# Residual add and RMSNorm: three shared slots of six rows in a hardware loop in place of two slots of eight rows unrolled

## The chip, the cores and the metric

The kernel runs on one core of one Trainium2 chip. The metric is the device time of one execution in microseconds (us). Every byte comes from the chip's memory (HBM) and goes back to it; the other cores are idle.

## The reference

```python
def reference(x, residual, gamma, eps):
    z = x + residual
    rms = np.sqrt(np.mean(z ** 2, axis=-1, keepdims=True) + eps)
    return (z / rms * gamma).astype(np.float32)
```

`x` and `residual` are float32 of 32 x 2048 x 2048, that is 65,536 rows of 2,048 numbers (8 KiB a row). The two inputs are 1,073.7 MB and the output is 536.9 MB. `gamma` is one row, all ones in the inputs used, but read and multiplied in.

## The kernel before, in words

The rows are cut into 64 tiles of 1,024 rows. Each of the 128 partitions of the on-chip memory (SBUF) takes 8 neighbouring rows of a tile, 64 KiB. There are three slots of that size: two, `z0` and `z1`, for x, z and the result in place, used in turn, and one, `r_slot`, for residual. With gamma (8 KiB) that is 200 KiB a partition.

One queue, that of SyncE (SP), issues all large transfers: residual of a tile whole (L58), x in two halves of four rows (L64), the store whole (L69), that of the last tile in halves (L73). The instructions of one queue are issued in program order, and each waits for its semaphores before it is issued, so one that waits holds up all behind it.

VectorE (DVE) adds four rows at once (L80). ScalarE (ACT) squares each row and sums it (L83), then takes the root (L90). VectorE inverts it (L94) and multiplies each row by it and by gamma (L97). The order in the main loop, unrolled by Python into one straight program, is: store of tile i-1, compute of tile i, residual of i+1, x of i+1. Residual can be loaded when both adds of the tile before are done; x when the store that empties its slot has landed.

## Time and profile before

| | |
|---|---|
| median of 10 runs | 3734.39 us (3733.63 to 3734.95) |
| profiled execution, its own time | 3735.05 us |
| its span, first to last instruction | 3733.3 us |
| bytes moved by the DMA engines | 1610.82 MB, mean 431 GB/s |
| busy: VectorE, ScalarE | 62%, 29% |
| q1, the queue issued from SP | 99.9% of 16 engines' span |

The page gives, for one profiled execution, each engine's busy time, the work of 40 equal slices, the DMA queues, the chain of work that ended last, and the costliest groups of instructions. In a group's row stand line, engine, operation and shapes, then busy time in us and the mean of one in ns, then the idle time ahead of it and what ended most of it. The view of waits gives for each waiting line who released it: us in total, times, longest. Behind the page lie the records of single DMA packets: start, duration, size. A packet here is one partition's share of one transfer; a transfer has 128, eight on each of the 16 DMA engines, and ends with one small semaphore write by each engine.

### The profile page before, as it was taken

How to read it: one execution, taken by the hardware profiler on the slowest of the kernel's cores; microseconds unless marked ns; L12 is line 12 of the kernel's file. 1: busy time of each engine (PE TensorE's matmuls, PEld its weight loads, DVE VectorE, ACT ScalarE, POOL GpSimd, SP SyncE). 2: the span in 40 equal slices, each digit the busy share in tenths (PEclk: the TensorE clock that was granted, in tenths of full speed). 3: DMA queues.
4: the chain of work that ended last, by engine and by line, in shares of the span. 5: the costliest groups of instructions: out<-in, count | busy, mean ns of one | idle time of the engine just before them, and what ended most of it. 6: DMA issues, size and time to landing. Idle time of an engine off the chain costs nothing.

```text
span 3733.3 us, 2427 instructions
## 1 busy us (share of the span) xinstructions
DVE 2297.9 (62%) x772; ACT 1066.0 (29%) x1154; POOL 0.2 (0%) x4
## 2 busy tenths in 40 slices
DVE  5665755657557565575655756657566575665756
ACT  2331322313223132231322313323233232331322
POOL 0000000000000000000000000000000000000000
DMA  9999999999999999999999999999999999999999
GB/s 424 413 433 431 434 436 430 436 432 434 434 430 438 432 433 433 430 437 432 433 434 431 436 432 432 437 429 436 431 433 435 431 436 433 430 436 434 433 435 388
DMA packets 37035, 1610.82 MB, mean 431 GB/s; under 512 B 4116, under 2 KB 4116, under 8 KB 4116
## 3 DMA queue, kind: packets, MB, share of 16 engines
q1 hardware_dynamic: 37008, 1610.63, 99.9%
q14 instruction: 19, 0.16, 0.0%
q10 hardware_dynamic: 8, 0.03, 0.0%
HBM read 1073.77 MB, written 536.87 MB: 431 GB/s over the span
## 4 chain that ended last, share of the span: by engine, by line
DMA 66%; another core or an unknown queue 16%; DVE 16%; SPq 1%; ACT 0%; issue 0%; DVEq 0%
DMA z<-in_x_dram 64%; DVE z L80 15%; DMA out_dram<-z 1%; DVE z L97 1%; DMA r_slot<-in_residual_dram 1%; SPq L64 1%; SPq L58 0%; ACT sq_junk L83 0%; DVE rstd L94 0%; DVEq L158 0%; ACT L90 0%; ACT rms L90 0%; DVEq L80 0%
## 5 line engine op out<-in xcount | busy, mean ns | idle before, releaser
L80 DVE TENSOR_TENSOR z<-z,r_slot 128x8192 f32<-128x8192 f32 x128 | 1112.5, 8692 | 1395.6 <-DMA z<-in_x_dram 1382.7
L83 ACT ACTIVATE sq_junk<-z 128x2048 f32<-128x2048 f32 x512 | 963.5, 1882 | 2636.0 <-DVE z L80 2623.9
L97 DVE SCALAR_TENSOR_TENSOR z<-z,rstd,gamma_tile 128x2048 f32<-128x2048 f32 x512 | 1169.9, 2347 | 4.5
L83 ACT ACTIVATION_READ_ACCUMULATOR sq_junk<-z 128x1 f32 x512 | 95.5, 186 | 0.0
L90 ACT ACTIVATE rms<-ssq,eps_tile 128x4 f32<-128x4 f32 x128 | 38.1, 297 | 4.1
L94 DVE RECIPROCAL rstd<-rms 128x4 f32<-128x4 f32 x128 | 21.8, 171 | 0.1
L113 DVE LOAD_MASK_SELECT gamma_tile<-gamma_tile x1 | 0.0, 14 | 21.3 <-DMA gamma_tile<-in_gamma_dram 21.3
L83 ACT ACT_TABLE_LOAD x1 | 1.3, 1283 | 4.4 <-issue 4.4
L113 DVE STREAM_SHUFFLE gamma_tile<-gamma_tile 128x2048 f32<-128x2048 f32 x1 | 2.4, 2418 | 0.0
L108 DVE MEMSET gamma_tile<- 128x2048 f32 x1 | 1.8, 1765 | 0.4 <-issue 0.4
L90 ACT ACT_TABLE_LOAD x1 | 1.3, 1283 | 0.0
L55 DVE MEMSET eps_tile<- 128x1 f32 x1 | 0.1, 59 | 0.8 <-PEq L144 0.8
L144 POOL MEMSET const-uint8-127<- 128x1 uint8 x1 | 0.1, 103 | 0.0
L144 POOL MEMSET const-bfloat16-1.0<- 128x1 bf16 x1 | 0.1, 102 | 0.0
L144 POOL MEMSET const-float32-0.0<- 128x1 f32 x1 | 0.1, 99 | 0.2 <-issue 0.2
L144 POOL MEMSET const-float32-1.0<- 128x1 f32 x1 | 0.1, 99 | 0.0
## 6 DMA issues: line engine op xcount, KB each, us to landing
z<-in_x_dram SPq DMA_DIRECT2D x128, 4096.0 KB, 38.3
out_dram<-z SPq DMA_DIRECT2D x2, 4096.0 KB
r_slot<-in_residual_dram SPq DMA_DIRECT2D x64, 29.9
out_dram<-z SPq DMA_DIRECT2D x63, 50.1
gamma_tile<-in_gamma_dram ACTq DMA_DIRECT2D x4, 8.0 KB
```

What stands on the lines that cost most here:

```text
L55: nc.vector.memset(eps_tile, float(eps))
L64: nc.sync.dma_start(out=z[:, s, :], in_=x_t[i][:, s, :])
L80: nc.vector.tensor_add(out=z[:, s, :], in0=z[:, s, :], in1=r_slot[:, s, :])
L83: nc.scalar.activation(out=sq_junk, in_=z[:, h * H + g, :], func=Act.Square, accum_out=ssq[:, g : g + 1],)
L90: nc.scalar.activation(out=rms, in_=ssq, func=Act.Sqrt, bias=eps_tile, scale=inv_d)
L94: nc.vector.reciprocal(out=rstd, in_=rms)
L97: nc.vector.scalar_tensor_tensor(out=row, in0=row, scalar=rstd[:, g : g + 1], in1=gamma_tile, op0=mult, op1=mult,)
L108: nc.vector.memset(gamma_tile, 0.0)
L113: nc.vector.stream_shuffle(gamma_tile, gamma_tile, [0] * 32)
L144: nc = _bacc.Bacc("TRN2", target_bir_lowering=False, num_devices=1)
```

## The change

- **Slots and tiles.** Four slots of 48 KiB a partition in place of three of 64 KiB: three (`z0` to `z2`) for x, z and result, one for residual. A tile is 768 rows, six a partition. 65,536 rows are 85 such tiles and 256 rows over; these make a first tile of two rows a partition. Its residual goes into `z2`, which is free then, so that tile 1's residual can go into `r_slot` at once.
- **Transfers.** x is loaded whole. Only the last tile is cut: its residual, its compute and its store go in three pieces of two rows.
- **Order.** For each tile: store of i-1, x of i+1, compute of i, residual of i+1. x is no longer behind residual on SP.
- **Compute.** Adds take three rows at once (128x6144), in two groups; roots and reciprocals are of three values.
- **A loop of the hardware.** Tiles 2 to 82 run in `For_i`, three tiles a pass, 27 passes. Addresses in HBM come from registers. With `iteration_sync="reg_based"` the loop's semaphores are never set back: each pass compares them with registers that grow by what one pass adds. Nine transfers in the body count on eight semaphores in turn, so DMAHW0 is used by the first (the store, L88) and the ninth (residual, L91). There is no barrier between passes; when the loop is left, SP waits for all transfers and all engines meet at one.

In the program as built, the first store of the body waits for DMAHW0 to hold 32 for every pass gone by (16 for each of the two transfers that count on it), beside VectorE's count for the rows scaled. The instructions of SP in the body are:

```
L88 DMACopy out_0_dram<-z1_65 128x12288 [waits DMAHW3,DMAHW0,DMAHW4,DVE,DMAHW6]
L89 DMACopy z0_64<-in_x_dram 128x12288 [waits DMAHW1]
L91 DMACopy r_slot_67<-in_residual_dram 128x12288 [waits DMAHW2,DVE]
L88 DMACopy out_0_dram<-z2_66 128x12288 [waits DMAHW0,DMAHW7,DVE]
L89 DMACopy z1_65<-in_x_dram 128x12288
L91 DMACopy r_slot_67<-in_residual_dram 128x12288 [waits DMAHW5,DMAHW2,DVE]
L88 DMACopy out_0_dram<-z0_64 128x12288 [waits DMAHW3,DMAHW1,DVE]
L89 DMACopy z2_66<-in_x_dram 128x12288
L91 DMACopy r_slot_67<-in_residual_dram 128x12288 [waits DMAHW5,DVE]
```

(Waits on semaphores of before the loop, which have been met since, and register instructions are left out.)

```diff
-    R = 8
-    H = R // 2
+    R = 6
+    NZ = 3
+    n_full = n_rows // (P * R)
+    left = (n_rows - n_full * P * R) // P
+    sizes = ([left] if left else []) + [R] * n_full
...
-    stats = ctx.enter_context(tc.tile_pool(name="stats", bufs=3))
+    stats = ctx.enter_context(tc.tile_pool(name="stats", bufs=6))
...
-    z_slots = [slots.tile([P, R, D], fp32, name=f"z{k}") for k in range(2)]
+    z_slots = [slots.tile([P, R, D], fp32, name=f"z{k}") for k in range(NZ)]
...
+    last = n_tiles - 1
+    piece = 2
+
+    def pieces(i):
+        k = sizes[i]
+        return [(a, min(a + piece, k)) for a in range(0, k, piece)] if i == last else [(0, k)]
+
+    def r_of(i):
+        return z_slots[NZ - 1] if i == 0 else r_slot
...
+    def cycle(i, at):
+        z_next = z_slots[(i + 1) % NZ]
+        nc.sync.dma_start(out=o_full[at - 1], in_=z_slots[(i - 1) % NZ])
+        nc.sync.dma_start(out=z_next, in_=x_full[at + 1])
+        compute(i)
+        nc.sync.dma_start(out=r_slot, in_=r_full[at + 1])
+
+    def load_x(i):
+        nc.sync.dma_start(out=z_slots[i % NZ][:, : sizes[i], :], in_=rows(x_f, i))
+
     def load_r(i):
-        nc.sync.dma_start(out=r_slot, in_=r_t[i])
-
-    def load_x(i):
-        z = z_slots[i % 2]
-        for h in range(2):
-            s = slice(h * H, (h + 1) * H)
-            nc.sync.dma_start(out=z[:, s, :], in_=x_t[i][:, s, :])
+        for a, b in pieces(i):
+            nc.sync.dma_start(out=r_of(i)[:, a:b, :], in_=rows(r_f, i)[:, a:b, :])
 
     def store(i):
...
+        for a, b in pieces(i):
+            nc.sync.dma_start(out=rows(o_f, i)[:, a:b, :], in_=z_slots[i % NZ][:, a:b, :])
...
     def compute(i):
...
+        if i == last:
+            before = None
+            for a, b in pieces(i):
+                add(i, a, b)
+                rms = square(i, a, b)
+                if before is not None:
+                    scale(i, *before)
+                before = (a, b, rms)
+            scale(i, *before)
             return
...
+        groups = [(a, min(a + 3, sizes[i])) for a in range(0, sizes[i], 3)]
+        rms_of = []
+        for a, b in groups:
+            add(i, a, b)
+            rms_of.append(square(i, a, b))
+        for (a, b), rms in zip(groups, rms_of):
+            scale(i, a, b, rms)
...
+    load_x(0)
     load_r(0)
-    load_x(0)
     load_gamma()
     load_x(1)
+    load_r(1)
     compute(0)
-    load_r(1)
-    for i in range(1, n_tiles):
+    def turn(i):
         store(i - 1)
+        if i + 1 < n_tiles:
+            load_x(i + 1)
         compute(i)
         if i + 1 < n_tiles:
             load_r(i + 1)
-            load_x(i + 1)
-    store(n_tiles - 1)
+
+    lo = 2
+    n_loop = (last - 1 - lo) // NZ
+    for i in range(1, lo):
+        turn(i)
+    with tc.For_i(0, n_loop * NZ, NZ, iteration_sync="reg_based") as iv:
+        for c in range(NZ):
+            cycle(lo + c, iv + (lo + c - first_full))
+    for i in range(lo + n_loop * NZ, n_tiles):
+        turn(i)
+    store(last)
```

The helpers `add`, `square` and `scale` hold what L80, L83 to L90 and L94 to L97 did, on rows a to b of a tile (L106, L112 and L119, L127 and L130 after).

## The prediction

> **What bounds the kernel now.** I read the page's head, its DMA rows, and the busy time by windows.

> ```profile
> span 3733.3 us, 2427 instructions
> DVE 2297.9 (62%) x772; ACT 1066.0 (29%) x1154; POOL 0.2 (0%) x4
> ...
> DMA  9999999999999999999999999999999999999999
> ...
> q1 hardware_dynamic: 37008, 1610.63, 99.9%
> ```

> The only full resource is the 16 DMA engines: q1's packets take 99.9% of their span. VectorE is busy 62%, ScalarE 29%. The windows view (length, busy time and instructions of each engine, clock, DMA share, GB/s; packets are counted where they start) says where the transfers stop:

> ```profile
> 163.38:3654.16 3490.78, 2150.01 (x721) 997.10 (x1080) 0.00 (x0) 1.00 1.00 433
> 100.20:101.80 1.60, 1.56 (x3) 1.40 (x4) 0.00 (x0) 1.00 0.01 0
> 3704.00:3712.00 8.00, 7.96 (x6) 6.46 (x9) 0.00 (x0) 1.00 0.13 57
> ```

> In 3490.78 us of steady state the share is 1.00 at 433 GB/s. There are two holes, at 100 us and ahead of the last stores. The second costs nearly nothing: by the trace's packet records one of the 16 engines lags further and further, ends the store of tile 62 at 3712.27 us and starts the last tile's at once, while the others have been idle since 3703.6 to 3710.9. The span is that engine's unbroken work. So what matters is any moment at which *all* engines have nothing queued. SP is the only issuer of these transfers, and its own waits are hidden behind transfers already queued:

> ```profile
> SPq L58 <- DVE rstd L94: 1772.7, 63, 29.5
> SPq L58 <- DMA r_slot<-in_residual_dram: 678.6, 62, 12.5
> SPq L64 <- DMA out_dram<-z: 625.7, 62, 10.5
> SPq L69 <- DVE z L97: 465.4, 63, 18.3
> ```

> The last row is the important one: the store (L69) waits for the scaled rows, never for a load.

> [...]

> **The change part by part.**

> *Bytes and packets.* Bytes are the same, 1610.63 MB. A 65,536-byte packet takes 2418 ns in the packet records, a 32,768-byte one 1213.5: about 9 ns plus 37.6 ns per KiB. So a 48 KiB packet should take 1816 ns. One tile before: 16 packets of 2418 and 16 of 1213.5 per engine, and four 9 ns semaphore writes, 58.14 us; times 64, 3721.0. After: three transfers of 8 x 1816 + 9, 43.61 us, times 85, 3706.9, plus 14.7 for the two-row tile, 3721.6. Difference +0.6; I take 0 (from -3 to +4, as packet times vary a little).

> *VectorE and ScalarE.* The costliest groups (line, engine, shapes, count; busy us, mean ns of one; idle before):

> ```profile
> L80 DVE TENSOR_TENSOR z<-z,r_slot 128x8192 f32<-128x8192 f32 x128 | 1112.5, 8692 | 1395.6 <-DMA z<-in_x_dram 1382.7
> L83 ACT ACTIVATE sq_junk<-z 128x2048 f32<-128x2048 f32 x512 | 963.5, 1882 | 2636.0 <-DVE z L80 2623.9
> L97 DVE SCALAR_TENSOR_TENSOR z<-z,rstd,gamma_tile 128x2048 f32<-128x2048 f32 x512 | 1169.9, 2347 | 4.5
> ```

> An add of 128x6144 is 6.52 us (8692 x 6144/8192). Per tile the two adds are 13.0, scaling 6 x 2.35 and two reciprocals 0.17 each: 27.5 us of the 43.6 that its transfers take. ScalarE: 6 squares of 1.88 and 0.19 for reading the sum, two roots of 0.30: 13. Both hide under the transfers, as do the other small statistics tiles and their larger number of buffers. Call T the landing of residual i: add done T+13.1, so residual i+1 is issued then; scaling done about T+27.5, so store i could be issued then. By FIFO the queue at T still holds store i-1 and x i+1 (29.0 us), then residual i+1 (to T+43.6). An unhindered store comes 16 us early. Order and slots alone leave no hole.

> *The loop.* This is where I choose. The body has nine transfers; the built program counts them on eight semaphores in turn, so the ninth (residual load, L91) and the next pass's first (store, L88) share one. In the instruction list that L88 waits for DMAHW0 to hold 32 per pass gone by, that is for *both* its predecessors: the last residual load must have landed. This is the newest transfer issued, so when the store is let go all 16 engines are empty. x, too (L89), stands behind the store on SP, so nothing fills the hole. The rows were scaled 16 us earlier, so that cover of 16 us is given away and a drain takes its place, once a pass: 26 times (27 passes; the counters' starting values let the first through). The other waits in the body name transfers that are at least one store and one load older, and pass at once.

> Price of one drain, from the trace: last packet to landing 0.37 to 0.47 us (records: the load of x that DVE starts on at 33.57 ended its last packet at 33.01, landed at 33.48); three combined waits ahead of the store, 0.06 us each as at the program's end, 0.2, and 0.05 to wake; issue to first store packet 0.84 to 0.99 (issued 3711.41, first packet 3712.25, last engine 3712.40). Sum 1.5 to 1.7. Unshown by the trace: a transfer whose address comes from a register, and the wait for the slowest of 16 engines in each pass. They can't be below 0; at most I give them 1.2 together: 0.6 for the slowest engine (the 16 parts of one landing near 142 us are 0.63 us apart) and 0.6 for addresses, about two issues of 0.33 (L58). I take 1.8 a drain: 26 x 1.8 = **46.8 us** (range 1.4 to 2.8: 36 to 73).

> The computed addresses stand ahead of the waits on SP and are hidden by them. Behind the waiting store on SP: x i+1, residual i+1. VectorE has no work anyway (it waits for the residual just landed), so the next residual still goes out at T+13, under 29 us of store and x. One drain, no echo.

> *Leaving the loop.* SP waits for all transfers, then a barrier of all engines. One more drain of 1.8, and a barrier: from the last landing (3732.26) to release (3732.75) it takes 0.5 at the program's end[...]. I take **3.0** (1.5 to 6[...]).

> *Start.* Loads of 4.9 + 4.9 + 14.5 + 14.5 us are queued at once, to about 41. Tile 0's store is ready at about 28 (its add from 12.5, gamma's shuffle and two scalings; if gamma is as late as in the trace, 24.3 us, at 32). Residual 2 follows add 1 at 55, while store 0 and x 2 run to 60.6. So the hole at 100 us (1.4) goes: **-0.7**, from 0 (the laggard skipped it) to -1.4.

> *End.* Residual pieces land 4.8 us apart; the store of tile 84 runs 14 us past the last, in which the pieces are added, squared and scaled (last piece ready at +18.3; the two earlier piece stores run to +23.8). No hole, but before had none on its slowest engine: **0**. Without the pieces' cover it would be 18 us.

> Sum: 3733.3 + 46.8 + 3.0 - 0.7 = 3782.4 span. The profiled execution took 3735.05, 1.75 over its span; the median of the runs, 3734.39, is 0.66 below it. So I expect 3782.4 + 1.1 = **3783.5 us**, 1.3% slower.

> **Rivals.**
> *A: no drain (not slower).* If the store at the top of the body goes out at T+27.5, or the queue otherwise never empties, only leaving the loop remains: 3734.4 + 3.0 - 0.7 = 3737, within 0.2%. It decides on whether the store waits past residual's last byte; it needs only 16 us. For it: before, stores wait for VectorE alone. Against: the count in the instruction list. With the laggard also re-aligned at each pass, and its 7 us lag recovered, 3730. Chance 0.06, of which 0.02 faster.
> *B: drain with a costly restart.* Register addresses[...], or a barrier put the price at 4 us: 26 x 4 + 6 = 110, 3843. For: none of these is in the trace. Against: the back-edge is taken 30 us before the wait ends. Chance 0.1.
> *C: packets of a register-addressed transfer are smaller.* The trace's 8,192-byte packets (instructions, gamma) take 309 ns, against 2418/8 = 302 for as many bytes of a 65,536-byte one, 2.2% more: +82 us on 3721, with drains 3865. For: only a register-addressed form is new. Against: 48 KiB per partition lies in one piece at both ends. Chance 0.04.

> The forecast has 0.8. The range 3765 to 3815 takes in drains of 1.1 to 3.0 us and leaves out A, B and C. What a measurement of this kernel can tell from no change is 0.2%, 7.5 us: slower 0.94, same 0.04, faster 0.02.

> **What would show it.** In the profile after: SP's waits with store L88 released by the residual's landing, about 26 times; in windows, holes of about 1.8 us every 132.6 us between 130 and 3640 us and a share of 1.00 between; the residual's landing about 43 us apart; VectorE about as busy as before; q1's packets near 33,500 data packets (262 transfers of 128) and 4,200 semaphore writes. If store L88 is released by VectorE, the forecast fails towards A; if holes are over 3 us, towards B; if packets number some 200,000, towards C.

## The result, and the profile after

The changed kernel takes 3842.48 us (median, 3840.11 to 3844.55) against 3734.34 us: 1.029 times the time before, 95% interval 1.0281 to 1.0299. The forecast was 3783.5, with a range of 3765 to 3815. So the direction was right and the size was wrong: 108 us were lost where 49 had been expected.

The page of the kernel after, head, DMA rows and costliest groups:

```profile
span 3841.8 us, 4931 instructions
DVE 2312.1 (60%) x860; ACT 1075.5 (28%) x1198; POOL 0.2 (0%) x4
...
q1 hardware_dynamic: 37728, 1610.63, 98.3%
...
q14 instruction: 1, 0.01, 0.0%
...
L106 DVE TENSOR_TENSOR z<-z,r_slot 128x6144 f32<-128x6144 f32 (+1 forms) x171 | 1107.5, 6517 | 1487.0 <-DMA r_slot<-in_residual_dram 1463.1
L112 ACT ACTIVATE sq_junk<-z 128x2048 f32<-128x2048 f32 x512 | 963.5, 1882 | 2739.4 <-DVE z L106 2720.2
L130 DVE SCALAR_TENSOR_TENSOR z<-z,rstd,gamma_tile 128x2048 f32<-128x2048 f32 x512 | 1173.7, 2347 | 6.1
```

The two compute engines do nearly the same work as before (VectorE 2312 us, before 2298). The bytes are the same and q1's packets fill 98.3% of a longer span in place of 99.9%. Note that 98.3% of 3841.8 is 3777 us, against 3730 before: part of the loss is not idle time but packets that take longer. In this text a packet is "drawn out" by the time that it takes beyond the usual time of a packet of its size.

SP's own waits (us in total, times, longest) show the predicted wait:

```profile
...
SPq L88 <- DMA r_slot<-in_residual_dram: 774.9, 26, 30.3
SPq L91 <- DVE rstd L127: 719.1, 54, 13.4
SPq L88 <- DVE z L130: 622.5, 55, 12.8
...
SPq L185 <- DMA r_slot<-in_residual_dram: 29.2, 1, 29.2
```

The store L88 is released by a landing of residual 26 times, once per back-edge (the jump from the end of a pass to the start of the next), and SP waits for one more at the loop's exit (L185). The wait of the other 55 stores of the loop ends with VectorE, as it did for the stores before.

What one such wait does is seen in windows (length, busy of each engine, clock, DMA share, GB/s) around the back-edge at 1291 us:

```profile
1290.10:1292.40 2.30, 0.79 (x1) 0.00 (x0) 0.00 (x0) 1.00 0.00 0
1307.00:1334.00 27.00, 11.84 (x7) 4.01 (x5) 0.00 (x0) 1.00 1.02 437
1354.00:1424.00 70.00, 38.94 (x17) 16.79 (x19) 0.00 (x0) 1.00 1.01 435
1302.00:1311.00 9.00, 8.81 (x5) 8.84 (x12) 0.00 (x0) 1.00 0.91 350
1331.00:1341.00 10.00, 2.18 (x1) 0.00 (x0) 0.00 (x0) 1.00 1.01 393
```

In the first row no packet starts for 2.3 us. The last two rows are what the forecast did not have: about 14 and 43 us after the restart the rate falls to 350 and 393 GB/s, although transfers are queued, as the timeline of SP (start, duration) shows. The x load (L89), the residual load (L91) and the next store (L88 at 1319.02) had each been issued well before the transfer ahead of it ended:

```profile
1291.65 0.36 SPq L88 DMA_DIRECT2D out_dram<-z  x1
1292.27 0.33 SPq L89 DMA_DIRECT2D z<-in_x_dram  x1
1304.76 0.33 SPq L91 DMA_DIRECT2D r_slot<-in_residual_dram  x1
1319.02 0.36 SPq L88 DMA_DIRECT2D out_dram<-z  x1
```

The falls are the first two places where the engines turn from writing to reading (store to x) and from reading to writing (residual to store). By the packet records the last 48 KiB packet before each turn takes about 2.6 to 2.7 us, as a mean of the engines, instead of 1.815. With the packet behind it, 0.88 us are drawn out at the first turn and 0.91 at the second. At the later turns of the same pass it is 0.1 or less.

Added up over all packets, an engine is idle 62.4 us longer in the profile after than in the unrolled kernel below, as a mean of the 16, and its packets are drawn out by 52.6 us more (over 1.815 us for 48 KiB and 0.611 for 16 KiB). The two make up the difference of the spans (3841.8 - 3726.8 = 115.0), as they must, since the transfers are the same: this splits the loss and does not explain it.

### The profile page after: what moved, and what is told of

It is laid out like the page before. It is cut to its first block, busy times and chain, and to the rows that moved or that the text cites. A ratio compares the mean times of both kernels' runs of the same rounds, so it can differ in the third digit from the quotient of the medians.

```text
span 3841.8 us, 4931 instructions
## 1 busy us (share of the span) xinstructions
DVE 2312.1 (60%) x860; ACT 1075.5 (28%) x1198; POOL 0.2 (0%) x4
## 2 busy tenths in 40 slices
DMA  9999999999999999999999999999999999999999
## 3 DMA queue, kind: packets, MB, share of 16 engines
q1 hardware_dynamic: 37728, 1610.63, 98.3%
## 5 line engine op out<-in xcount | busy, mean ns | idle before, releaser
L106 DVE TENSOR_TENSOR z<-z,r_slot 128x6144 f32<-128x6144 f32 (+1 forms) x171 | 1107.5, 6517 | 1487.0 <-DMA r_slot<-in_residual_dram 1463.1
L112 ACT ACTIVATE sq_junk<-z 128x2048 f32<-128x2048 f32 x512 | 963.5, 1882 | 2739.4 <-DVE z L106 2720.2
L130 DVE SCALAR_TENSOR_TENSOR z<-z,rstd,gamma_tile 128x2048 f32<-128x2048 f32 x512 | 1173.7, 2347 | 6.1
L112 ACT ACTIVATION_READ_ACCUMULATOR sq_junk<-z 128x1 f32 x512 | 95.4, 186 | 0.0
L119 ACT ACTIVATE rms<-ssq,eps_tile 128x3 f32<-128x3 f32 (+1 forms) x172 | 51.0, 296 | 5.5
L127 DVE RECIPROCAL rstd<-rms 128x3 f32<-128x3 f32 (+1 forms) x172 | 29.6, 172 | 12.0 <-ACT rms L119 12.0
L106 DVE TENSOR_TENSOR z<-z,z 128x4096 f32<-128x4096 f32 x1 | 4.4, 4424 | 11.5 <-DMA z<-in_residual_dram 11.5
## 6 DMA issues: line engine op xcount, KB each, us to landing
r_slot<-in_residual_dram SPq DMA_DIRECT2D x84, 6144.0 KB, 30.7
```

The lines of the kernel that those rows point to most:

```text
L106: nc.vector.tensor_add(out=z[:, a:b, :], in0=z[:, a:b, :], in1=r_of(i)[:, a:b, :])
L112: nc.scalar.activation(out=sq_junk, in_=z_slots[i % NZ][:, a + g, :], func=Act.Square, accum_out=ssq[:, g : g + 1],)
L119: nc.scalar.activation(out=rms[:, :n], in_=ssq[:, :n], func=Act.Sqrt, bias=eps_tile, scale=inv_d)
L127: nc.vector.reciprocal(out=rstd[:, :n], in_=rms[:, :n])
L130: nc.vector.scalar_tensor_tensor(out=row, in0=row, scalar=rstd[:, g : g + 1], in1=gamma_tile, op0=mult, op1=mult,)
```

## The experiments

Two theories stood against each other. **Drain:** each back-edge empties and restarts the DMA engines, and all of its price of 4.15 us comes from that (the 25 periods between 210.11 and 3584.73, the issue of L88, are 134.98 us each; the transfers of three tiles take 130.83). **Loop machinery:** the part above the 1.6 us of receipt and issue is due to addresses from registers, fetches or the branch. The diffs show the lines that matter. From the third run on, the kernel is the unrolled one, and the diff of the restart with x first is against the drains without a loop.

### The loop written out

```diff
-    with tc.For_i(0, n_loop * NZ, NZ, iteration_sync="reg_based") as iv:
-        for c in range(NZ):
-            cycle(lo + c, iv + (lo + c - first_full))
-    for i in range(lo + n_loop * NZ, n_tiles):
+    for i in range(lo, n_tiles):
         turn(i)
```

> The changed kernel with its loop written out by Python, everything else kept. Drain theory (all of the loss comes from the 26 drains at the back-edge and the one at the exit): no drain is left, so 3728 to 3736 us, no hole in the transfers between 10 and 3800 us. Rival (the loss lies in the tiles: 48 KiB packets, six rows, order of the queue): about 3840.

Measured: 3728.58 us, 0.9984 of the kernel before (0.9978 to 0.9991). All of the loss is in the loop, none in the slots, tiles or order. The page, and SP's waits:

```profile
span 3726.8 us, 2716 instructions
...
q1 hardware_dynamic: 37728, 1610.63, 100.0%
```

```profile
SPq L102 <- DVE z L130: 1192.5, 87, 20.9
```

87 waits of the stores (L102) end with VectorE, and q1 fills the span. The steady state by windows, of the unrolled kernel and then of the changed one with its loop:

```profile
163.00:3654.00 3491.00, 2164.14 (x801) 1008.86 (x1120) 0.00 (x0) 1.00 1.00 433
```

```profile
1211.00:3583.00 2372.00, 1425.81 (x529) 665.38 (x742) 0.00 (x0) 1.00 0.98 420
```

433 GB/s is the rate of the kernel before; the loop takes it to 420. The unrolled version is the fastest of the three, by 0.16% against the kernel before; the ranges of their runs do not overlap.

### The loop kept, with ten transfers in a pass

```diff
-        nc.sync.dma_start(out=z_next, in_=x_full[at + 1])
+        if i == lo:
+            nc.sync.dma_start(out=z_next[:, :3, :], in_=x_full[at + 1][:, :3, :])
+            nc.sync.dma_start(out=z_next[:, 3:, :], in_=x_full[at + 1][:, 3:, :])
+        else:
+            nc.sync.dma_start(out=z_next, in_=x_full[at + 1])
```

> The loop kept, but one x load of each pass is cut in two, so a pass has ten transfers and the next store shares its semaphore with an x load that is older than the last residual. Shared-semaphore theory: no drain at the back-edge, one at the exit, 3733 to 3741 us. Rival (loop machinery: register addresses, branch, instruction fetch): still about 3840.

Measured: 3733.70 us, 0.9998 (0.9989 to 1.0006). The store still waits 26 times for a load, but for x:

```profile
SPq L88 <- DMA z<-in_x_dram: 391.9, 26, 15.1
SPq L90 <- DMA r_slot<-in_residual_dram: 359.6, 26, 14.2
```

When x lands, residual is still queued behind it, 13.8 us of it on average (359.6 over 26). When the first x load of the next pass (L90) then waits for that residual, the store is queued, and q1's packets fill 99.9% of the span. Register addresses, the branch and the barrier at the exit are all still there. So it is the shared semaphore, and only through emptying the queue. What remains against the unrolled kernel, 5.1 us, goes with the exit and the 27 more transfers. By the packets' times the added transfers take 2.2 us of it, and two turns behind the exit are drawn out by 0.9 us each.

### Drains without a loop

In the unrolled kernel, every third tile (26 in all), two one-element operations on VectorE make the store and the x load depend on the residual just landed. The first adds residual times zero to an element of z, the second writes an element that x then overwrites.

```diff
+    def wait_for_residual(i):
+        r = r_of(i)[:, R - 1, D - 1 : D]
+        z = z_slots[(i - 1) % NZ][:, R - 1, D - 1 : D]
+        nc.vector.scalar_tensor_tensor(
+            out=z, in0=r, scalar=0.0, in1=z, op0=mult, op1=mybir.AluOpType.add
+        )
+        nc.vector.tensor_copy(out=z_slots[(i + 1) % NZ][:, R - 1, D - 1 : D], in_=r)
+
     def turn(i):
+        if 5 <= i <= 80 and i % 3 == 2:
+            wait_for_residual(i)
         store(i - 1)
```

> The unrolled kernel, in which every third tile's store and x load wait for the residual just landed, by two one-element operations on VectorE: 26 drains and no loop. If the whole price of a drain, 4.15 us a pass in the changed kernel, comes from emptying and restarting the DMA engines: 26 x 4.1 above the unrolled kernel, 3832 to 3845 us, with the last store packets ahead of x and the last residual packets drawn out as in the changed kernel. If the part above the 1.6 us of receipt and issue belongs to the loop: 26 x 1.7 above it, about 3775.

Measured: 3837.53 us, 1.0275 (1.0259 to 1.0291). That is 108.95 us above the unrolled kernel, 4.19 a drain, as much as in the loop (4.15). The row of its waits that carries it:

```profile
SPq L102 <- DVE z L179: 792.3, 26, 30.9
```

Packets are drawn out as in the loop: 0.8 us at the turn near 1302 us and 1.0 at the one near 1331. No loop machinery is needed for the price.

### The same wait with one transfer queued behind

The copy is left out, so x does not wait, and the scheduler moves x ahead of the store.

```diff
-        nc.vector.tensor_copy(out=z_slots[(i + 1) % NZ][:, R - 1, D - 1 : D], in_=r)
```

> As the kernel with drains unrolled, but x alone does not wait, and the scheduler puts it ahead of the store: the store waits for the residual's landing just as long, with one 14.5 us transfer queued behind that residual. Drain theory: the wait costs nothing while something is queued, 3728 to 3740 us. Rival (the late store itself costs): about 3770 or more.

Measured: 3729.28 us, 0.9987 (0.9980 to 0.9993), 0.7 above the unrolled kernel, though SP waits nearly as long. The second fence shows x ahead of such a store:

```profile
SPq L102 <- DVE z L176: 751.5, 26, 28.9
```

```profile
1226.51 0.33 SPq L94 DMA_DIRECT2D z<-in_x_dram  x1
1255.82 0.34 SPq L102 DMA_DIRECT2D out_dram<-z  x1
```

Compare its row of waits with that of the run before: 26 waits of 29 us against 26 of 30. One set costs 0.7 us, the other 109. Here the length of a wait says nothing of its cost; what is queued behind the awaited transfer does.

### A drain at every tile

`i % 3 == 2` is dropped: 76 drains.

> The unrolled kernel with a drain at each of 76 tiles in place of every third. If all packets drawn out belong to the turnarounds between writing and reading that the engines make in step after a restart (about 0.8 us where store gives way to x, about 1.0 where residual gives way to store): only the first of the two is left in a tile, since the drain stands in place of the second, and the engines have less time to spread, so about 1.6 + 0.3 + 0.8 = 2.7 a drain, 76 x 2.7 + 3728.6 = 3930 to 3950 us. If a drain has one fixed price of 4.15: 76 x 4.15 + 3728.6 = 4044.

Measured: 3940.23 us, 1.0552 (1.0536 to 1.0567), as the theory of turns had it: 211.65 us above the unrolled kernel, 2.78 a drain. SP's waits count the drains, one of them released by the other operation:

```profile
SPq L102 <- DVE z L179: 2471.3, 75, 33.6
...
SPq L102 <- DVE z L176: 32.9, 1, 32.9
```

The price of a drain was not the same in the two runs: 2.78 with 76, 4.19 with 26. Here the engines end residual 0.39 us apart (median), against 1.10 with 26 drains, so less is lost in waiting for the slowest. Only the turn from store to x is left before the next drain, about 0.9 us drawn out in the records. An engine is idle 140 us longer than in the unrolled kernel, 1.8 a drain, against 2.2 with 26.

### Half-size packets at the two turns

The four transfers after a drain go in halves of three rows, and the one-element operations touch both halves.

```diff
+    def halves(out, in_):
+        for h in (slice(0, 3), slice(3, 6)):
+            nc.sync.dma_start(out=out[:, h, :], in_=in_[:, h, :])
```

> The unrolled kernel with 26 drains, where the four transfers after a drain (store, x, residual, next store) go in halves of three rows, so that packets at the two turnarounds are of 24 KiB. The shorter packets' own overhead of about 9 ns each adds 26 x 4 x 8 x 9 ns = 7.5 us to 3837.5. If what a turnaround in step costs is about half a packet (0.9 us of 1.8 here, 1.1 of 2.4 in the kernel before at 75 and 138 us): 0.9 less a drain, 3837.5 + 7.5 - 23 = 3815 to 3828 us. If it is a fixed time per turnaround: 3840 to 3848.

Measured: 3847.76 us, 1.0305 (1.0288 to 1.0322), at the upper end of the range given for a fixed time. The 24 KiB packets are drawn out by about 0.9 us at each of the two turns after 1292 us. So what a turn cost here did not go with the size of its packets: about 0.9 us with 24 KiB, 0.9 and 1.0 with 48 KiB.

### The store cut by partitions

Meant to put the engines out of step before the first turn, so that the 16 do not make it at the same moment: the store after a drain goes in four pieces, of 112 partitions, of 16 (four rows), of 12 and of 4 (two rows).

```diff
+    def store_staggered(i):
+        o, z = rows(o_f, i), z_slots[i % NZ]
+        nc.sync.dma_start(out=o[:112], in_=z[:112])
+        nc.sync.dma_start(out=o[112:, :4, :], in_=z[112:, :4, :])
+        nc.sync.dma_start(out=o[112:124, 4:, :], in_=z[112:124, 4:, :])
+        nc.sync.dma_start(out=o[124:, 4:, :], in_=z[124:, 4:, :])
```

> The unrolled kernel with 26 drains, where the store after a drain is cut by partitions so that the DMA engines end it out of step[...]. In-step theory: the drawn-out packets at the next two turnarounds mostly vanish, 0.6 - 1.5 a pass, about 3837 - 26 x 0.9 = 3800 to 3820 us. Rival (a turnaround costs the same however the engines stand): 3837 + 26 x 0.6 = 3853.

Measured: 3923.48 us, 1.0507 (1.0491 to 1.0523), far above both figures. The run decides nothing. The 0.6 us a pass in both figures is my estimate of what the slowest engine carries more, by the 0.611 us of a 16 KiB packet; which engines took which piece was not shown. The piece of 16 partitions did not depend on the one-element operation and was issued 21 us ahead of the others (1432.29 against 1453.41 us), and the packets of the store were drawn out all through it, about 0.5 us in every 3 from 1452 to 1473 us, as those of 128 partitions in the changed kernel are not (0.06 us or less in each of the first seven packets, as a mean of the engines). The experiment changed more than it was meant to.

### The restart with x first

```diff
+        nc.vector.tensor_copy(out=z_slots[(i + 1) % NZ][:, R - 1, D - 1 : D], in_=r)
+        load_x(i + 1)
         nc.vector.scalar_tensor_tensor(
             out=z, in0=r, scalar=0.0, in1=z, op0=mult, op1=mybir.AluOpType.add
         )
-        nc.vector.tensor_copy(out=z_slots[(i + 1) % NZ][:, R - 1, D - 1 : D], in_=r)
```

> The unrolled kernel with 26 drains, restarted with the x load and then the store. In-step theory: a load restarts with first packets drawn out by 0.7 us, as at the kernel's start, and then come turnarounds in step as before: 4.1 to 4.8 a drain, 3837 to 3855 us. If what is drawn out is bound to a store being the first transfer: packets at later turnarounds are not drawn out, about 2.9 a drain, 3800.

Measured: 3878.34 us, 1.0387 (1.0370 to 1.0404): 5.8 a drain, above both. An engine's idle time over the unrolled kernel is 3.6 us a drain, against 2.2 with the store first. Medians over the 26 drains: the load's first packet starts 0.95 us after its issue but that of the last engine 1.89 (store: 0.84 and 0.99), and the engines had ended 2.6 us apart. The first packets are drawn out by 0.75 us, and the last ones before the turn from x to store by 1.25; the next turns, from store to residual and from residual to store, cost nothing (0.05 or less).

This speaks against the engines' step as the cause of drawn-out turns. In this run they start the packet ahead of the costly turn 1.7 us apart (median). In the changed kernel the costly turns have them 0.15 and 0.4 us apart, but the next two, with 0.7 and 1.0, cost 0.03 or less. So here a turn between engines 1.7 us apart cost 1.25 us, more than the 0.9 and 1.0 of those in step. The unrolled kernel, too, starts with loads, and there, too, the first turn alone is drawn out much, by 0.6 us near 40 us.

## Why the prediction was wrong

- **What bounds, and bytes and packets: right.** A 48 KiB packet takes 1815 ns (predicted 1816), and residual lands 30.7 us after its issue (median), where the order of the queue gave 30.5 (from T+13.1 to T+43.6). The term of 0 us for tiles and -0.7 for the start fell 5 us short of the gain: unrolled, they give -5.9. The packets of the kernel before are drawn out by about 8 us an engine, those of the unrolled kernel by 5.2, and the hole at 100 us is gone.
- **The loop: right in place, number and cause.** 26 drains at L88 and one at the exit, by residual's landing; ten transfers in a pass end those at L88, and the exit's remains.
- **The 1.5 to 1.7 us from last packet to first packet: right.** Medians over the drains: last packet of all engines to landing 0.37, landing to issue 0.25, issue to first store packet 0.85, to that of the last engine 1.00. Together 1.5 to 1.6. Register addresses, given up to 0.6, cost nothing: issue to first packet is 0.85 with them and 0.84 in the unrolled kernel with drains.
- **The failed step: "I take 1.8 a drain".** It measured 4.15: the 26 drains cost 107.9 us where 46.8 were taken. Two terms were too small or missing. The engines end the last residual 1.3 us apart (median), so the average engine is idle 2.4 us in the hole, not 1.6; I had allowed up to 0.6 for the slowest engine and taken 0.2 for it and the addresses together. And the two turns after a restart draw packets out by about 0.9 and 1.0 us, for which I had nothing. The evidence was in the records of the kernel before: its packets are drawn out by 1.1 us between 75 and 80 us and by 1.1 near 138 us, and hardly at later turns (0.12 near 195 and 255). I had read the restart up to its first packet and stopped there.
- **"One drain, no echo": right for the queue, wrong for the rate.** No second hole follows, but the two turns draw packets out while the queue is full.
- **Leaving the loop: 3.0 taken.** The parts worked out from the trace make 2.3 of it (a drain's 1.8 and the 0.5 of the program's end); the rest was my estimate. In the changed kernel the exit's hole is 3.3 us on average over the engines, of which landing to issue 1.11, and the two turns behind it draw packets out by 1.7: together 5.0.
- **Rival B gave 3843, and the time is 3842.48, but for other reasons.** Its costly addresses and barrier do not show at the back-edge, nor do fetches of instructions: q14 has one packet in the whole span, at 3721 us, behind the loop's exit. The kernel with ten transfers has the same register addresses and the same branch, at no cost there. That a number fits is not evidence for its story. Rivals A and C fell: the waits, and 37,728 packets.

With the measured terms: 3837.5, the unrolled kernel with 26 drains, + 5.0 for the exit = 3842.5.

**Open:** why turns soon after a restart cost and later ones do not. With the store first, the cost falls together with the engines being in step (first packets of the store within 0.15 us of each other) and is gone as these spread. The run meant to break the step decided nothing, and in the run with x first a turn with the engines 1.7 us apart cost more. That the turns cost is measured; the cause is not shown, and the step alone is not it.

## What to carry to other kernels

In a kernel bound by transfers, ask of each wait on the issuing queue not how long it is but what is queued behind the transfer it waits for: 26 waits of 29 us cost 0.7 us with one transfer behind, and 26 of 30 us cost 109 with none. In a loop whose semaphores are used in turn, count the transfers of a pass against the semaphores: here nine on eight tied the first store to the newest load, and a tenth transfer freed it. Price a drain to the point where the rate is back, not to the first packet: of the 4.15 us here, 2.4 lay ahead of the first packet and 1.8 at the two turns about 14 and 43 us behind it.

## What the runs showed of the hardware that was not expected

- After the idle moment of a drain (2.4 us in the changed kernel, mean of the engines), the first turn from store to load and the next from load to store drew packets out by about 0.9 and 1.0 us, with packets of 24 and of 48 KiB nearly alike; later turns cost 0.03 us or less (medians in the changed kernel). After a restart with a load, one turn alone cost, 1.25 us (0.05 or less at the next two).
- A restart with a load was slower than with a store: the last engine's first packet came 1.89 us after issue (median) against 0.99.
- A store in pieces of 112, 16, 12 and 4 partitions had packets drawn out all through, by about 0.5 us in every 3; the run does not tell which piece does it.
- A transfer with its address from registers started as fast as one with a fixed address (0.85 and 0.84 us from issue).
